# One diffusion-layer kernel: modulation of all tokens straight out of PSUM, the later modulation loads on GpSimd's queue, and more buffers for the stores of gates and values

## The chip, the cores and the metric

The kernel runs on one core of one Trainium2 chip. Five engines work side by side, each through its own list of instructions in order: PE (matrix multiplications and transposes, with PEld, the load of its stationary operand), DVE (vector), ACT (scalar, activations), POOL (GpSimd) and SP, which here only issues transfers. Transfers run on 16 DMA engines. The metric is the device time of one execution in microseconds, the median of several runs. Times inside a profile count from the start of the profiled span.

## The reference, cut to what matters

One layer of a diffusion backbone over 1024 latent tokens and 256 context tokens, in fp32. What the change touches is the front of the layer:

```python
mod_lat = (silu(c) @ w_ada + b_ada)[:, None, :]
mod_ctx = silu(c_ctx) @ w_ada + b_ada
sh1, sc1, gt1, sh2, sc2, gt2 = split(mod_lat, 6, axis=-1)
csh1, csc1, ... = split(mod_ctx, 6, axis=-1)
h_lat = rms_norm(x, norm_mix_g) * (1 + sc1) + sh1
h_ctx = rms_norm(ctx, norm_mix_g) * (1 + csc1) + csh1
y_lat, _ = token_mixer(h_lat, h_ctx, ...)   # h @ w_in -> attention and gated linear attention
x = x + gt1 * y_lat
x = x + gt2 * hier_moe(rms_norm(x, norm_ffn_g) * (1 + sc2) + sh2)
```

The projection h @ w_in gives, among other columns, the values of the gated linear attention (gv), its low-rank gates, keys and queries, the output gate r, and the values of the differential attention (dv).

## The kernel before, in words

Tokens stand in ten tiles of 128 (two of context, eight of latents), two to a pair: five pairs, pair 0 the context. An fp32 product is done as three matmuls of split operands (mm3, lines 119 to 121: high times high, low times high, high times low), so every weight w is split into whi (ACT, L275) and wlo (DVE, L276), and the modulated tokens, transposed to have the model dimension on partitions, into hThi and hTlo. A unit of work is one tile of tokens against one 256-column block of w_in: 24 matmuls into one of three PSUM tiles named acc.

The stages in order of time:

1. Modulation. The first 2048 columns of w_ada come as 16 pieces of 512 KB (wada, L385, SP's queue, AW = 4 buffers); ACT makes wadh (L390), DVE wadl (L391), PE multiplies (L397); ACT or DVE copy the rows out of PSUM (L406, L408), PE transposes them (L410), DVE forms modT (L435 to L437). Beside it, start_chain normalises pair 0 (its scaling is L340 on POOL), transposes it and copies the transposes from PSUM into xn (L315 on ACT, L317 on DVE).
2. Values. For each pair: squares (L297, ACT), the reciprocal root (L105 to L113, small steps of ACT and DVE), the scaling of the token tiles (L303, POOL), PE transposes in eight (L312), copies into xn (L317), and for each of eight blocks k of 128 model dimensions the modulation, done twice: ACT writes the rounded hThi (L324), POOL writes it unrounded over xn (L325), DVE subtracts (hTlo, L326). Then 20 units of gv: ACT copies acc out (gvs, L469) and SP's queue stores it (L470).
3. klr: keys and low-rank gates, 10 units.
4. r and q: 16 units of the output gate (gs, L703 to L709, stored at L710) and 8 of queries (ki, L723, which needs a load eP, L719; transposes L659). Beside it ada_rest computes the other 4096 columns of the modulation: 64 loads aw of 256 KB (L603, SP's queue, three buffers), one DVE step each which accumulates w times silu(c) into aacc (L645, L647), and for every 512 columns finish(j): the split of aacc into ah (ACT, L613) and al (DVE, L614), two matmuls against ones (L617, L618), the addition of the bias row brow (DVE, L619), and stores. The recurrence over the states sall (L589, L590) runs on DVE.
5. dv: 20 units whose result goes out as dqh (ACT, L864) and dql (DVE, L865), two buffers each, both stored from SP's queue. Then the rotary units, attention, output projection and the mixture of experts, up to the end at 1442 us.

The order on PE, ACT, DVE and POOL is written out by the program: chains are generators whose yields carry a delay (the table DEL), and a "Weave" lets them step when the unit loop has ticked that much. So an edit in a chain moves its instructions against those of the units. Transfers stand in the order in which their queue's engine reaches them; a load that waits for a free buffer holds what is queued behind it on that queue.

## Time and profile before

| | us |
|---|---|
| median of 3 runs | 1440.54 (1439.92 to 1441.53) |
| the profiled execution | 1444.24 |
| its span | 1442.4 |
| PE busy in the span | 1331.0 |
| DVE busy | 1115.2 |
| ACT busy | 870.6 |
| POOL busy | 298.7 |
| mean granted clock of PE | 0.967 |

The profile lists busy time by engine, groups of instructions by line, waits (which instruction stood idle until which other one ended) and a timeline. A share of busy time over the whole span is an average over stages with different limits, and so the windows by stage are to be read first. A granted clock of 1.00 is PE's upper level of 2.4 GHz, 0.50 the lower of 1.2 GHz.

### The profile page before, as it was taken

How to read it: one execution, taken by the hardware profiler on the slowest of the kernel's cores; microseconds unless marked ns; L12 is line 12 of the kernel's file. 1: busy time of each engine (PE TensorE's matmuls, PEld its weight loads, DVE VectorE, ACT ScalarE, POOL GpSimd, SP SyncE). 2: the span in 40 equal slices, each digit the busy share in tenths (PEclk: the TensorE clock that was granted, in tenths of full speed). 3: DMA queues.
4: the chain of work that ended last, by engine and by line, in shares of the span. 5: the costliest groups of instructions: out<-in, count | busy, mean ns of one | idle time of the engine just before them, and what ended most of it. 6: DMA issues, size and time to landing. Idle time of an engine off the chain costs nothing.

```text
span 1442.4 us, 21048 instructions
## 1 busy us (share of the span) xinstructions
PE 1331.0 (92%) x7352; PEld 1104.1 (77%) x7352; DVE 1115.2 (77%) x1653; ACT 870.6 (60%) x1458; POOL 298.7 (21%) x273
## 2 busy tenths in 40 slices
...
GB/s 262 202 96 150 199 220 186 249 244 183 175 174 178 265 152 18 141 36 112 220 254 138 263 311 355 375 368 369 373 372 377 374 368 354 366 371 359 347 294 151
DMA packets 121538, 360.76 MB, mean 250 GB/s; under 512 B 18726, under 2 KB 47422, under 8 KB 98388
## 3 DMA queue, kind: packets, MB, share of 16 engines
...
q8 instruction: 59, 0.97, 0.3%
q14 instruction: 51, 0.42, 0.1%
...
## 4 chain that ended last, share of the span: by engine, by line
PE 68%; DVE 13%; DMA 7%; ACT 5%; issue 4%; POOL 2%; SPq 0%; ACTq 0%; POOLq 0%; DVEq 0%
PE acc L119 5%; PE acc L120 5%; PE acc L121 5%; PE y L119 4%; PE y L121 4%; PE y L120 4%; PE u L120 4%; PE g L120 4%; PE u L121 4%; PE g L121 4%; PE g L119 4%; PE u L119 4%; PE y L1678 4%; DVE nm L1039 3%; PE S L1034 2%
## 5 line engine op out<-in xcount | busy, mean ns | idle before, releaser
L1630 DVE TENSOR_TENSOR lo<-ring,hi 128x1024 fp32r<-128x1024 f32 x323 | 382.5, 1221 | 42.5 <-ACT hi L1629 28.3
L1629 ACT ACTIVATE hi<-ring 128x1024 fp32r<-128x1024 f32 x323 | 335.7, 1059 | 86.9 <-PE y L121 54.2
L119 PE MATMUL acc<-whi,hThi 128*128 128x256 f32 (+1 forms) x592 | 175.6, 297 | 5.5 <-DVE dql L865 3.9
L121 PE MATMUL acc<-whi,hTlo 128*128 128x256 f32 (+1 forms) x592 | 170.0, 287 | 0.9 <-DVE hTlo L326 0.6
L120 PE MATMUL acc<-wlo,hThi 128*128 128x256 f32 (+1 forms) x592 | 169.9, 287 | 0.4 <-DVE wlo L276 0.3
L119 PEld LDWEIGHTS acc<-whi,hThi 128*128 128x128 f32 x592 | 115.2, 195 | 6.8 <-DVE dql L865 4.3
L120 PEld LDWEIGHTS acc<-wlo,hThi 128*128 128x128 f32 x592 | 114.9, 194 | 2.1 <-DVE wlo L276 0.8
L121 PEld LDWEIGHTS acc<-whi,hTlo 128*128 128x128 f32 x592 | 114.5, 193 | 2.4 <-DVE hTlo L326 2.1
L119 PE MATMUL g<-hi,xh 128*128 128x512 f32 x256 | 103.9, 406 | 0.1
L120 PE MATMUL u<-lo,xh 128*128 128x512 f32 x256 | 100.5, 393 | 3.1 <-DVE lo L1630 3.1
L119 PE MATMUL u<-hi,xh 128*128 128x512 f32 x256 | 100.6, 393 | 2.0 <-ACT hi L1629 2.0
L120 PE MATMUL g<-lo,xh 128*128 128x512 f32 x256 | 101.1, 395 | 0.8 <-DVE lo L1630 0.8
L121 PE MATMUL g<-hi,xl 128*128 128x512 f32 x256 | 101.2, 395 | 0.0
L121 PE MATMUL u<-hi,xl 128*128 128x512 f32 x256 | 100.3, 392 | 0.0
L1039 DVE TENSOR_REDUCE nm<-S 128x1 f32<-128x1280 f32 x64 | 94.8, 1484 | 6.1 <-PE S L1034 6.0
L1034 PE MATMUL S<-kst,qst 128*128 128x512 f32 (+1 forms) x384 | 92.0, 377 | 6.6 <-ACT p L1044 5.5
L1044 ACT ACTIVATE p<-S,nm 128x1280 f32<-128x1280 f32 x64 | 85.1, 1329 | 16.3 <-DVE nm L1039 11.1
L119 PE MATMUL y<-hi,th 128*128 128x512 f32 x186 | 85.2, 458 | 0.0
L1034 PEld LDWEIGHTS S<-kst,qst 128*128 128x128 f32 x384 | 65.3, 192 | 19.5 <-ACT p L1044 9.6
L1609 POOL DMA_INDIRECT xg<-dr_h,tok x32 | 45.1, 1411 | 151.7 <-ACT hi L1629 129.3
L121 PE MATMUL y<-hi,tl 128*128 128x512 f32 x186 | 72.6, 390 | 0.0
L120 PE MATMUL y<-lo,th 128*128 128x512 f32 x186 | 72.5, 390 | 0.0
...
## 6 DMA issues: line engine op xcount, KB each, us to landing
...
```

The lines of the kernel that those rows point to most:

```text
L119: nc.tensor.matmul(out_ap, ah, bh, start=start, stop=False)
L120: nc.tensor.matmul(out_ap, ah, bl, start=False, stop=False)
L121: nc.tensor.matmul(out_ap, al, bh, start=False, stop=stop)
L1034: nc.tensor.matmul(S[:, c0:c0 + cn], st["qst"][m][s][:, qt * P:(qt + 1) * P], st["kst"][m][:, c0:c0 + cn], start=(s == 0), stop=(s == 1))
L1039: nc.vector.tensor_reduce(d["nm"][:, m:m + 1], d["S"][m], AX.X, OP.max, negate=True)
L1044: nc.scalar.activation(d["p"][m], d["S"][m], AF.Exp, bias=d["nm"][:, m:m + 1], accum_out=d["sm"][:, m:m + 1])
L1609: nc.gpsimd.indirect_dma_start(out=xgb[e % 3], out_offset=None, in_=dr_h2, in_offset=bass.IndirectOffsetOnAxis(ap=tok[:, o:o + 1], axis=0) ...
L1629: nc.scalar.activation(hi, raw, AF.Copy)
L1630: nc.vector.tensor_tensor(lo, raw, f32(hi), op=OP.subtract)
L1678: nc.tensor.matmul(y[:, n], tf[:, kk - PARTS], ws[kk][:, n * 512:(n + 1) * 512], start=start, stop=stop)
```

## The change

- The loads of the first modulation part have 6 buffers (AW), the token tiles xt 6 (4 before).
- xn and its copies are gone. pair_transpose puts two blocks k of both tiles into one PSUM tile; DVE (36 times) or ACT (4 times, even k of pair 0) modulates from there into xm; pair_parts then copies xm into hThi on ACT and subtracts on DVE, both 512 wide. Pair 0 is transposed and modulated at the start of the value stage, behind modT.
- The scaling of the token tiles (L303) goes from POOL to ACT. The squares of pair 1 stand before rows 2 and 3 of the modulation, its scaling before the chains of the other pairs.
- The 64 loads aw are issued by GpSimd. In finish, the bias row is loaded there (one buffer), and a yield stands between ah and al.
- The small memset of st goes to DVE; gs has 4 buffers instead of 2; dqh and dql have 3, and in the dv stage two units share one, so that six units have room.

The first hunk, left out here, only sets AW from 4 to 6.

```diff
--- before.py
+++ after.py
...
@@ -283,11 +283,11 @@
     ada = ip.enter_context(ExitStack())
     ap = ada.enter_context(tc.tile_pool(name="ada", reuse_waits="tile", bufs=1))
     wv = io["w_ada"].rearrange("(p k) j -> p k j", k=KD)
-    xts, ssqs, xns = {}, {}, {}
+    xts, ssqs = {}, {}
 
     def tile_load(t):
         src = io["ctx"][t * P:(t + 1) * P] if t < NL else io["x"][(t - NL) * P:(t - NL + 1) * P]
-        xts[t] = ap.tile([P, D], F32, name="xt", bufs=4)
+        xts[t] = ap.tile([P, D], F32, name="xt", bufs=6)
         nc.sync.dma_start(xts[t], src)
 
     def tile_square(t):
@@ -297,33 +297,37 @@
         nc.scalar.activation(junk, xts[t], AF.Square, accum_out=ssqs[t // 2][:, t % 2:t % 2 + 1])
 
     def pair_scale(g):
-        *_, r = rsqrt(ap, ssqs[g], 1.0 / D, [P, 2], "n1")
+        *_, r = rsqrt(ap, ssqs[g], 1.0 / D, [P, 2], f"n1{g % 2}")
         for i in range(2):
             t = 2 * g + i
-            nc.gpsimd.tensor_scalar(xts[t], xts[t], r[:, i:i + 1], 1.0, op0=OP.mult, op1=OP.mult)
-
-    def tile_transpose(t, hb):
-        g = t // 2
-        if t % 2 == hb == 0:
-            xns[g] = ap.tile([P, KD, 256], F32, name="xn", bufs=3)
-        pt = pp.tile([P, 512], F32, name="t", bufs=DEL["T"])
-        for b in range(4):
-            k = hb * 4 + b
-            nc.tensor.transpose(pt[:, b * P:(b + 1) * P], xts[t][:, k * P:(k + 1) * P], ident)
-        dst = xns[g][:, hb * 4:hb * 4 + 4, t % 2 * P:t % 2 * P + P]
-        if hb and t < 4:
-            nc.scalar.activation(dst, pt.rearrange("p (b c) -> p b c", b=4), AF.Copy)
+            nc.scalar.activation(xts[t], xts[t], AF.Copy, scale=r[:, i:i + 1])
+
+    def modulated(g, k, dst, src):
+
+        c = 1 if 2 * g < NL else 0
+        sc, sh = modT[:, 1, k, c:c + 1], modT[:, 0, k, c:c + 1]
+        if g == 0 and k % 2 == 0:
+            nc.scalar.activation(dst, src, AF.Identity, scale=sc, bias=sh)
         else:
-            nc.vector.tensor_copy(dst, pt.rearrange("p (b c) -> p b c", b=4))
-
-    def pair_modulate(g, k):
-        c = 1 if 2 * g < NL else 0
-        sl = slice(2 * g * P, (2 * g + 2) * P)
-        sc, sh = modT[:, 1, k, c:c + 1], modT[:, 0, k, c:c + 1]
-        xn = xns[g][:, k]
-        nc.scalar.activation(hThi[:, k, sl], xn, AF.Identity, scale=sc, bias=sh)
-        nc.gpsimd.tensor_scalar(xn, xn, sc, sh, op0=OP.mult, op1=OP.add)
-        nc.vector.tensor_tensor(hTlo[:, k, sl], xn, f32(hThi[:, k, sl]), op=OP.subtract)
+            nc.vector.tensor_scalar(dst, src, sc, sh, op0=OP.mult, op1=OP.add)
+
+    def pair_transpose(g, kp):
+
+        pt = pp.tile([P, 2, 256], F32, name="t", bufs=DEL["T"])
+        for j in range(2):
+            for t in range(2):
+                k = 2 * kp + j
+                nc.tensor.transpose(pt[:, j, t * P:(t + 1) * P], xts[2 * g + t][:, k * P:(k + 1) * P], ident)
+        xm = ap.tile([P, 2, 256], F32, name="xm", bufs=2)
+        for j in range(2):
+            modulated(g, 2 * kp + j, xm[:, j], pt[:, j])
+        return xm
+
+    def pair_parts(g, kp, xm):
+
+        ks, sl = slice(2 * kp, 2 * kp + 2), slice(2 * g * P, (2 * g + 2) * P)
+        nc.scalar.activation(hThi[:, ks, sl], xm, AF.Copy)
+        nc.vector.tensor_tensor(hTlo[:, ks, sl], xm, f32(hThi[:, ks, sl]), op=OP.subtract)
 
     def start_chain():
 
@@ -339,29 +343,23 @@
         for t in range(2):
             nc.gpsimd.tensor_scalar(xts[t], xts[t], r[:, t:t + 1], 1.0, op0=OP.mult, op1=OP.mult)
         yield
-        yield
-        for t in range(2):
-            for hb in range(2):
-                tile_transpose(t, hb)
-                yield
 
     normed = [1]
 
     def pair_chain(g):
-        for t in (2 * g, 2 * g + 1):
-            tile_square(t)
-        pair_scale(g)
-        yield DEL["p0" if g > 1 else "pf"]
-        for t in (2 * g, 2 * g + 1):
-            for hb in range(2):
-                tile_transpose(t, hb)
-                yield DEL["p1" if g > 1 else "ph"]
-            if t + 4 < NA:
-                tile_load(t + 4)
-        for k in range(KD):
-            pair_modulate(g, k)
-            if k % 2:
-                yield DEL["p2" if g > 1 else "pg"]
+        if g > 1:
+            for t in (2 * g, 2 * g + 1):
+                tile_square(t)
+            pair_scale(g)
+            yield DEL["p0"]
+        for kp in range(KD // 2):
+            xm = pair_transpose(g, kp)
+            yield DEL["p1" if g > 1 else "ph"]
+            pair_parts(g, kp, xm)
+            yield DEL["p2" if g > 1 else "pg"]
+        for t in (2 * g + 6, 2 * g + 7):
+            if t < NA:
+                tile_load(t)
         normed[0] = g + 1
 
     with tc.manual_schedule():
@@ -430,16 +428,14 @@
                 next(wgen)
         for _ in chain:
             pass
+        for t in (2, 3):
+            tile_square(t)
         for n in range(2, 4):
             row(n)
         nc.vector.tensor_tensor(modT, pt[:, :, :, :2], bcol[:, :, :, None].to_broadcast([P, 2, KD, 2]), op=OP.add)
         nc.vector.tensor_tensor(modT, pt[:, :, :, 2:], modT, op=OP.add)
         nc.vector.scalar_tensor_tensor(modT[:, 1], modT[:, 1], 1.0,
                                        ncol[:, :, None].to_broadcast([P, KD, 2]), op0=OP.add, op1=OP.mult)
-        for k in range(KD):
-            pair_modulate(0, k)
-            if k % 2 and k < KD - 1:
-                next(wgen)
     dbg("modT", modT)
 
 
@@ -472,6 +468,13 @@
 
     side = Weave(DEL["w1"])
     with tc.manual_schedule(engines=COMPUTE):
+        for kp in range(KD // 2):
+            pair_parts(0, kp, pair_transpose(0, kp))
+            if kp < KD // 2 - 1:
+                next(wgen)
+        for t in (6, 7):
+            tile_load(t)
+        pair_scale(1)
         for g in range(1, NA // 2):
             side.add(pair_chain(g))
         for t0, t1 in ((0, 2), (2, 4), (4, NA)):
@@ -600,17 +603,20 @@
             i = len(ws)
             if i < 8 * KD:
                 ws.append(sp.tile([P, 512], F32, name="aw", bufs=3))
-                nc.sync.dma_start(ws[i], wv[:, i % KD, 2048 + i // KD * 512:2048 + (i // KD + 1) * 512])
+                nc.gpsimd.dma_start(ws[i], wv[:, i % KD, 2048 + i // KD * 512:2048 + (i // KD + 1) * 512])
 
         for _ in range(3):
             load()
         accs = {}
 
         def finish(j):
-            acc, brow = accs.pop(j)
+            acc = accs.pop(j)
+            brow = sp.tile([1, 512], F32, name="brow", bufs=1)
+            nc.scalar.dma_start(brow, io["b_rest"][:, j * 512:(j + 1) * 512])
             ah = sp.tile([P, 512], F32R, name="ah", bufs=1)
             al = sp.tile([P, 512], F32R, name="al", bufs=1)
             nc.scalar.activation(ah, acc, AF.Copy)
+            yield DEL["ar2"]
             nc.vector.tensor_tensor(al, acc, f32(ah), op=OP.subtract)
             yield DEL["ar2"]
             ps = pp.tile([P, 512], F32, name="t", bufs=DEL["T"])
@@ -635,9 +641,7 @@
 
         for j in range(8):
             acc = sp.tile([P, 512], F32, name="aacc", bufs=2)
-            brow = sp.tile([1, 512], F32, name="brow", bufs=2)
-            accs[j] = (acc, brow)
-            nc.scalar.dma_start(brow, io["b_rest"][:, j * 512:(j + 1) * 512])
+            accs[j] = acc
             for k in range(KD):
                 w = ws[j * KD + k]
                 c = sil[:, 0, k:k + 1]
@@ -687,7 +691,7 @@
             if t == 0:
                 nc.scalar.preload_act_table_set("natural_log_exp_and_others")
             st = sp.tile([P, 98], F32R, name="st", bufs=3)
-            nc.gpsimd.memset(f32(st[:, 96:98]), 1.0)
+            nc.vector.memset(f32(st[:, 96:98]), 1.0)
             nc.scalar.activation(st[:, 0:32], ps[:, 256:288], AF.Copy)
             nc.scalar.activation(st[:, 64:96], ps[:, 256:288], AF.Copy)
             nc.vector.tensor_tensor(st[:, 32:64], ps[:, 256:288], f32(st[:, 0:32]), op=OP.subtract)
@@ -699,7 +703,7 @@
         for i in range(2):
             for t in range(NT):
                 ps = bform(f"r{i}", NL + t)
-                gs = sp.tile([P, 256], F32, name="gs")
+                gs = sp.tile([P, 256], F32, name="gs", bufs=4)
                 nc.scalar.activation(gs, ps[:, :256], AF.Exp, scale=-1.0)
                 nc.scalar.activation(gs, gs, AF.Ln, bias=1.0)
                 nc.scalar.activation(gs, gs, AF.Exp, scale=-1.0)
@@ -805,8 +809,8 @@
 
     def evacuate(h, qk, c0, cn, ps):
 
-        hi = sp2.tile([P, 512], F32R, name="dqh")[:, :cn]
-        lo = sp2.tile([P, 512], F32, name="dql")[:, :cn]
+        hi = sp2.tile([P, 512], F32R, name="dqh", bufs=3)[:, :cn]
+        lo = sp2.tile([P, 512], F32, name="dql", bufs=3)[:, :cn]
         sc = 1.0 if qk else 0.125
         src = ps[:, :cn]
         if c0:
@@ -859,8 +863,9 @@
         for i in range(2):
             for t in range(NA):
                 ps = bform(f"dv{i}", t)
-                hi = sp2.tile([P, 512], F32R, name="dqh")[:, :256]
-                lo = sp2.tile([P, 512], F32, name="dql")[:, :256]
+                if t % 2 == 0:
+                    pair = [sp2.tile([P, 512], dt, name=nm, bufs=3) for nm, dt in (("dqh", F32R), ("dql", F32))]
+                hi, lo = [x[:, t % 2 * 256:t % 2 * 256 + 256] for x in pair]
                 nc.scalar.activation(hi, ps[:, :256], AF.Copy)
                 nc.vector.tensor_tensor(lo, ps[:, :256], f32(hi), op=OP.subtract)
                 nc.sync.dma_start(dr_v[i][0][:, t], f32(hi))
```

**ACT at the end of the modulation stage.** Before (wadh is a piece's high part, xn the copied transposes of pair 0, junk the squares of pair 1, wada the copied rows of the modulation):

```order
L390 ACTIVATE wadh<-wada 128x1024 x3
L315 ACTIVATE xn<-t 128x4x128
L390 ACTIVATE wadh<-wada 128x1024 x2
L315 ACTIVATE xn<-t 128x4x128
L390 ACTIVATE wadh<-wada 128x1024 x7
L406 ACTIVATE wada<-acc 4x512
L275 ACTIVATE whi<-wraw 128x512
L406 ACTIVATE wada<-g 4x512
L297 ACTIVATE junk,ssq<-xt 128x1024 x2
```

After:

```order
L388 ACTIVATE wadh<-wada 128x1024 x12
L404 ACTIVATE wada<-acc 4x512
L275 ACTIVATE whi<-wraw 128x512
L297 ACTIVATE junk,ssq<-xt 128x1024 x2
L404 ACTIVATE wada<-g 4x512
L310 ACTIVATE xm<-t,modT 128x256
```

The two xn copies between the wadh steps are gone, and the two squares moved ahead of the second copy of a row.

**PE at the start of the value stage.** Before (acc_474 is the first unit, acc_544 the second; t the transposes, here of pair 1):

```order
L119 MATMUL acc_474<-whi_449,hThi_154 128x256
L120 MATMUL acc_474<-wlo_450,hThi_154 128x256
L121 MATMUL acc_474<-whi_449,hTlo_155 128x256
L119 MATMUL acc_544<-whi_412,hThi_154 128x256
L120 MATMUL acc_544<-wlo_413,hThi_154 128x256
L121 MATMUL acc_544<-whi_412,hTlo_155 128x256
L312 MATMUL t_549<-ident_60,xt_356 128x128 x4
L119 MATMUL acc_544<-whi_412,hThi_154 128x256
```

After (xt_189 is of pair 0; xt_331 and xt_333 are pair 1; acc_485 is the first unit):

```order
L320 MATMUL t_460<-ident_60,xt_189 128x128
L119 MATMUL acc_485<-whi_387,hThi_154 128x256
L120 MATMUL acc_485<-wlo_388,hThi_154 128x256
L121 MATMUL acc_485<-whi_387,hTlo_155 128x256
L320 MATMUL t_489<-ident_60,xt_331 128x128
L320 MATMUL t_489<-ident_60,xt_333 128x128
L320 MATMUL t_489<-ident_60,xt_331 128x128
L320 MATMUL t_489<-ident_60,xt_333 128x128
L119 MATMUL acc_485<-whi_387,hThi_154 128x256
```

The first transposes of pair 1 moved from behind 27 unit matmuls to behind three.

**DVE from the last ki to the first dql.** Before (brow is the addition of a bias row):

```order
L723 TENSOR_TENSOR ki<-eP,acc 128x512
L645 SCALAR_TENSOR_TENSOR aacc<-aw,sil,aacc 128x512
L614 TENSOR_TENSOR al<-aacc,ah 128x512
L619 TENSOR_TENSOR brow<-t,brow 1x512
L645 SCALAR_TENSOR_TENSOR aacc<-aw,sil,aacc 128x512 x3
L614 TENSOR_TENSOR al<-aacc,ah 128x512
L619 TENSOR_TENSOR brow<-t,brow 1x512
L754 COPY st_in<-sall 64x512
L755 COPY st_in<-sall 64x512
L865 TENSOR_TENSOR dql<-acc,dqh 128x256
```

After:

```order
L727 TENSOR_TENSOR ki<-eP,acc 128x512
L625 TENSOR_TENSOR brow<-t,brow 1x512
L637 SCALAR_TENSOR_TENSOR ah<-brow,al 1x64x8
L649 SCALAR_TENSOR_TENSOR aacc<-aw,sil,aacc 128x512 x3
L651 TENSOR_SCALAR aacc<-aw,sil 128x512
L649 SCALAR_TENSOR_TENSOR aacc<-aw,sil,aacc 128x512 x4
L620 TENSOR_TENSOR al<-aacc,ah 128x512
L625 TENSOR_TENSOR brow<-t,brow 1x512
L649 SCALAR_TENSOR_TENSOR aacc<-aw,sil,aacc 128x512 x3
L620 TENSOR_TENSOR al<-aacc,ah 128x512
L625 TENSOR_TENSOR brow<-t,brow 1x512
L758 COPY st_in<-sall 64x512
```

Eleven steps of aacc now stand between the last ki and the first dql, where four stood.

## Rows read from the trace of the kernel before

**Rows 1.** Windows by stage: length, busy us (instructions) of PE, PEld, DVE, ACT, POOL; clock, DMA

```profile
20.00:43.60 23.60, 17.08 (x74) 6.20 (x72) 15.72 (x19) 14.09 (x19) 0.23 (x1) 0.92 0.84 292
43.60:122.00 78.40, 72.09 (x550) 69.12 (x551) 38.01 (x87) 42.36 (x93) 40.77 (x51) 0.89 0.41 129
...
186.00:288.00 102.00, 87.91 (x713) 83.62 (x713) 86.13 (x144) 41.43 (x90) 1.95 (x3) 0.97 0.72 220
288.00:475.00 187.00, 183.51 (x1122) 162.99 (x1121) 104.47 (x240) 47.58 (x145) 46.96 (x32) 0.99 0.62 191
```

**Rows 2.** Waits, modulation stage: who waited for whom; total us, times, longest

```profile
DVE wadl L391 <- ACT wadh L390: 5.9, 5, 2.2
ACT xn L315 <- PE t L312: 5.9, 2, 4.4
```

**Rows 3.** Timeline of DVE, modulation stage: start, us, line, instruction, [idle before]

```profile
28.34 3.63 DVE L391 TENSOR_TENSOR wadl<-wada,wadh 128x1024 fp32r<-128x1024 f32 x3 [0.99 <-ACT wadh L390]
...
38.40 1.23 DVE L391 TENSOR_TENSOR wadl<-wada,wadh 128x1024 fp32r<-128x1024 f32 x1 [0.20 <-ACT wadh L390]
...
43.35 0.17 DVE L437 SCALAR_TENSOR_TENSOR modT<-modT,c_ncol 128x16 f32<-128x16 f32 x1
```

**Rows 4.** Groups by line, value stage: instructions xcount | busy us, mean ns | idle before

```profile
L325 POOL TENSOR_SCALAR xn<-xn,modT 128x256 f32<-128x256 f32 x40 | 30.8, 784 | 31.8 <-ACT hThi L324 31.8
L324 ACT ACTIVATE hThi<-xn,modT 128x256 fp32r<-128x256 f32 x40 | 20.8, 588 | 0.0
...
L317 DVE COPY xn<-t 128x512 f32<-128x512 f32 x14 | 9.3, 685 | 3.1 <-PE t L312 3.1
```

**Rows 5.** Timeline of ACT at the end of the modulation stage

```profile
41.23 1.04 ACT L297 ACTIVATE junk<-xt 128x1024 f32<-128x1024 f32 x1
```

**Rows 6.** Timeline of POOL in the value stage

```profile
45.76 6.32 POOL L325 TENSOR_SCALAR xn<-xn,modT 128x256 f32<-128x256 f32 x6 [0.17 <-ACT hThi L324]
...
95.35 6.19 POOL L325 TENSOR_SCALAR xn<-xn,modT 128x256 f32<-128x256 f32 x8 [1.02 <-ACT hThi L324]
```

**Rows 7.** Timeline of PE where the second pair's transposes begin

```profile
54.27 1.11 PE L312 MATMUL t<-ident,xt 128*128 128x128 f32 x4 [0.46 <-POOL xt L303]
```

**Rows 8.** Windows at low granted clock (columns as in rows 1)

```profile
44.00:56.70 12.70, 11.14 (x39) 9.09 (x40) 6.22 (x18) 9.07 (x22) 9.86 (x10) 0.50 0.24 68
84.00:87.40 3.40, 3.40 (x18) 3.40 (x18) 1.04 (x2) 1.75 (x4) 2.42 (x4) 0.50 0.14 43
```

**Rows 9.** Waits in the stage of gates and queries

```profile
PE t L618 <- DVE al L614: 5.1, 4, 2.6
...
PE t L617 <- ACT ah L613: 2.9, 3, 1.5
```

**Rows 10.** Timeline of DVE around the last ki and the first dql

```profile
278.21 0.69 DVE L723 TENSOR_TENSOR ki<-eP,acc 128x512 f32<-128x512 f32 x1 [2.58 <-DMA eP<-dr_eP]
...
282.93 0.75 DVE L645 SCALAR_TENSOR_TENSOR aacc<-aw,sil,aacc 128x512 f32<-128x512 f32 x1 [0.16 <-DMA aw<-in_w_ada_dram]
...
287.10 0.42 DVE L865 TENSOR_TENSOR dql<-acc,dqh 128x256 f32<-128x256 f32 x1
...
295.40 0.43 DVE L865 TENSOR_TENSOR dql<-acc,dqh 128x256 f32<-128x256 f32 x1 [6.35 <-ACT dqh L864]
```

**Rows 11.** Timeline of SP's queue in the same stretch

```profile
279.58 0.33 SPq L603 DMA_DIRECT2D aw<-in_w_ada_dram  x1
```

**Rows 12.** Line 161: a plain load issued by GpSimd (durations min/median/max, ns)

```profile
L161 POOL DMA_DIRECT2D ring<-in_w_up_dram x1: 614/614/614, 823.2 to 823.2; - x1
```

**Rows 13.** Line 1609, GpSimd's gathers: time to landing

```profile
DMA to landing us min/median/max: 5.2/12.2/13.5
```

**Rows 14.** Waits in the first units of dv

```profile
PE acc L119 <- DVE dql L865: 3.9, 2, 2.6
```

2 lines of the change are left out of this document (1 added, 1 removed).

## The prediction, made before the changed kernel ran

> **What bounds the kernel now.** I read the table by stage first [rows 1]: PE is busy 72.09 of the 78.40 us of the value stage, 87.91 of the 102.00 us of the stage of gates and queries (r and q), and 183.51 of 187.00 us behind that. So nothing the diff does before 288 us changes what comes after; it only moves it. The places where time can come or go are the 23.60 us ahead of the value stage, in which neither PE (17.08) nor DVE (15.72) nor ACT (14.09) is full and the DMA engines are at 0.84; the value stage's start; and r/q, where DVE is busy 86.13 us, almost as much as PE, so that taking away a wait of PE alone buys little there.
>
> The times: the profiled execution took 1444.24 us with a span of 1442.4; the median of the three timed runs is 1440.54. All terms below are differences inside the span, and I add their sum to the median. A difference of 0.2% (2.9 us) is about what a measurement of this kernel can tell from none.
>
> **The modulation's first part (A).** The list of waits [rows 2] shows ACT standing 5.9 us in front of two copies of transposes (L315), one of them 4.4, with the next wadh behind it, and DVE waiting 5.9 us for wadh. Undisturbed, DVE does three pieces in 3.63 us, 1.21 each [rows 3]; its last piece starts at 38.40 and modT is ready at 43.52. The change takes the two ACT copies, their two DVE twins (0.685 each) [rows 4] and the transposes out of this stretch, and gives the loads six buffers. At most that is 5.9 + 2 x 0.685 = 7.3 us for the last piece; the nine pieces that DVE starts behind 23 us, at 1.22 each, would end near 34.5 instead of 39.6, 5.1 us less, and the DMA share of 0.84 says that the loads can hardly give more. Against it, the two squares of pair 1 (L297, 1.04 us each [rows 5]) now stand ahead of ACT's second copy of a modulation row, on the path to modT: +0.3 to +1.2, since PE's transposes of the row before run beside the first. I take **-4.7**, with -6 (squares hidden) and -3 (loads landing too late for six buffers to matter fully) as ends.
>
> **The value stage (B).** What the change removes is large and lies beside other work: 40 modulations on GpSimd (30.8 us), 40 ACT writes (20.8) [rows 4], 8 scalings on GpSimd and 40 DVE subtractions. In their place stand 36 modulations on DVE and 4 on ACT, 20 ACT copies and 20 DVE subtractions of double width, and 8 scalings on ACT (a 128x1024 ACT pass is 1.04 [rows 5]). ACT comes out a few us lighter, DVE one or two heavier, each still near half busy. So what counts is the path. Before, the first pair went at GpSimd's pace: six of its eight steps in 6.32 us [rows 6], the pair done 9 us after modT. After, each of four steps is ACT's modulation and copy, DVE's subtraction and split of a weight, then the next one: 0.6 + 0.6 + 0.7 + 0.7, with overlap 2.3 or so, the fourth done 8.8 us after modT. No gain.
>
> The second pair is worse placed. Before, its transposes stand behind 27 matmuls, and waited 0.46 us for the scaled tokens at 54.27, 10.75 us after modT [rows 7]. After, they stand behind three. The scalings wait on ACT behind the whole first pair, two small ACT steps with three of DVE between, and take 1.04 each: done 11.6 to 12.3 us after modT. There PE stands with 21 matmuls of its first unit behind it: at the half clock of that stretch (0.50; elsewhere at 0.50 PE did 18 in 3.40 us, 0.19 each [rows 8]) they are 4.0 us, at the full one 2. Later pairs repay some, since GpSimd no longer holds DVE's subtractions (PE ran at half clock from 84 to 87.4 us behind one such wait [rows 8]). Pairs that come 12.6 us apart make the last pair ready about 60.4 us after modT, against 58.5 (GpSimd's last step of it ends at 101.54 [rows 6], and one subtraction of DVE follows), with seven units behind it either way. I take **+4**; ends +1 (only the later transposes, the rest repaid) and +7 (all 21 matmuls at half clock and half the later gap again). A and B together are about -0.7: the start's gain is handed back by a pair 1 that is scaled too late.
>
> **Gates and queries (D).** The loads aw leave SP's queue, where each waited for its buffer and held the stores and loads behind it. On GpSimd's queue only the two zeroings (L853, L855) stand behind the 64 loads, and their first reader comes with the dv stage: nothing. On PE the new yield between ah and al covers the 5.1 and 2.9 us that L618 and L617 waited [rows 9]. But those were waits on a DVE that is nearly full; PE freed of them meets DVE's ki and gs a little later. What remains is DVE's own count. The order puts 43 accumulations of aacc between the first gate and the first dql, before 40, and 7 additions of brow, before 6: 3 x 0.68 + 0.6 = **+2.6**. The wait of ki for eP (2.58 us [rows 10]) had its load queued among aw loads on SP; it goes: **-2.6**.
>
> Then the tail. Before, 8.9 us lie between the last ki (278.21) and the first dql (287.10), with four accumulations [rows 10]. After, eleven stand there, eight in a row. They are the unknown of this change, for three buffers turn no faster than a load comes: on SP, the load that was issued at 279.58, as its buffer came free [rows 11], was waited for and used at 282.93 [rows 10]: 3.35 us. With three buffers a clump runs at (R + 0.74)/3 us a piece, R being that round trip: 1.37 instead of 0.74, times eight is 5.0 us, less some 2 us in which al and brow fill the wait. So **+3** at SP's R. The trace has two plain loads issued by GpSimd, which took 0.6 us of that engine [rows 12], which is below 0.74 and so no limit; and gathers of 512 KB which landed after 5.2 us at the least [rows 13]. R = 2.25 gives 0, R = 5.2 gives +8: the ends. I take SP's value, as the nearest row of the same size and layout.
>
> The Trainium skill, "DMA: Bandwidth & Descriptors", section "Anatomy of one DMA — SWDGE (gpsimd) path", gives 2.0 us plus bytes at 436 GB/s; by that estimate 256 KB would take 2.6 us, the tail would cost +1 instead of +3, and the forecast would be 2 us lower. No run here shows it.
>
> **Values (E).** The units of dv stored through two buffers; DVE stood 6.35 us and the first dql after it came at 295.40 [rows 10], PE having waited 2.6 us for one [rows 14]. Six units of room cover that: **-2.6**. What is late next is PE itself, full from there on [rows 1].
>
> **Clock (F).** PE will stand longer at one place, about 10 us in front of the fourth dv unit, whose PSUM buffer the first dql frees. After its gap before 84 us PE ran 3.4 us at 0.50 [rows 8], which at full clock would be 1.7. I take **+1.5**, 0 to 3.4. The klr stage keeps its order: 0, plus or minus 1.
>
> Sum: -4.7 + 4 + 2.6 - 2.6 + 3 - 2.6 + 1.5 = +1.2, so 1440.5 + 1.2 = **1441.7 us**.
>
> **The rivals.**
> Faster (1): pair 1's scaling is not what PE waits for, or is repaid at once (B = +1), and the loads land at R = 2.25 to 2.6 (tail 0 to +1). Then -4.7 + 1 - 2.6 + 0.5, with D's 2.6 against 2.6 and no clock loss, is -5.8; with a half of PE's 8 us at L617 and L618 paid back it is -10. About 1433. For it: each wait named was real in the trace. Against it: DVE's 86 of 102 us.
>
> Slower (2): loads issued by GpSimd come back late. At R = 4 us the tail costs +4.7 and the sum is +2.9, the point from which this case decides; at 5.2 it is +8, and the accumulations spread over r/q, which lie 1.5 to 2 us apart, wait as well above R = 4.5: some +3. 1441.7 - 3 + 8 + 3 is about 1450. For it: the gathers' 5.2 [rows 13]; against it: they run among the weight streams. The Trainium skill, "SBUF — State Buffer", section "Who interferes with whom", speaks for it: DVE copies and tensor_scalar in a two-port mode block GpSimd's writing of descriptors until they end. By rows here few such instructions stand in the tail (one start of an accumulator per eight), so alone it is a delay of half a microsecond.
>
> Not what it says (3): the first stage is paced by its DMA, and six buffers and freer engines bring 1.5 us instead of 4.7. Then 1445.
>
> **How the numbers follow.** The balance as summed, 1437.5 to 1446: 0.43; rival 1: 0.26; rival 2: 0.23; rival 3: 0.08. Of the balance, 0.29 lies within 0.2%, 0.03 below and 0.11 above; rival 1 is faster but for 0.02; rival 2 slower but for 0.02; rival 3 splits 0.02 and 0.06. Faster 0.27, same 0.35, slower 0.38. The range reaches into rivals 1 and 2 to about their middles: 1432 to 1451; the likeliest case alone is 1437.5 to 1446.
>
> **What would show it.** In the profile after: modT ready near 39 us (A; near 42 speaks for rival 3); PE idle before the first pair-1 transposes, and the last gvs some 81 to 83 us after modT (B; 78 or less refutes it); no wait of PE at L618 and none of ki for eP (D); waits of aacc for DMA aw bunched in the last 18 us before the first dql, and the time from a buffer's release to its next use: 3.3 us for me, under 2.6 for rival 1, over 4 for rival 2; no 6 us hole before a dql in dv (E); a half-clock stretch near 290 (F). The prediction is wrong if r/q shortens with PE, by more than 4 us, or if the first dql comes before 283 us or after 292.

## The result, and the profile after

The changed kernel is slower: 1454.10 us in the median of six runs (1448.37 to 1456.43) against 1440.59 before. The ratio is 1.0078 with a 95% interval of 1.0060 to 1.0096, that is 11.2 us; the two medians lie 13.5 us apart. Its profiled execution took 1451.38 us with a span of 1449.6. Forecast were 1441.7 us, 1.2 above before, with a range of 1432 to 1451 and a chance of 0.38 for slower.

Table by stage of the changed kernel, cut at its own places: behind modT, at the last gvs, the last ki, the first dql and the first score of the attention (columns as in [rows 1]):

```profile
20.00:39.60 19.60, 14.44 (x69) 5.04 (x66) 14.43 (x16) 13.40 (x16) 2.42 (x4) 0.96 0.93 330
39.60:125.70 86.10, 71.31 (x557) 68.98 (x558) 42.92 (x90) 43.80 (x83) 1.08 (x2) 0.89 0.35 111
189.50:279.60 90.10, 78.06 (x633) 74.26 (x631) 75.40 (x127) 37.51 (x82) 17.16 (x32) 0.97 0.66 205
279.60:300.70 21.10, 11.46 (x85) 9.86 (x83) 12.94 (x20) 4.94 (x10) 6.19 (x11) 0.82 0.60 191
300.70:483.90 183.20, 181.85 (x1113) 162.09 (x1114) 103.67 (x239) 45.71 (x141) 45.30 (x31) 0.99 0.62 195
```

Set beside the kernel before, the profiled times of the same events say where the time went:

| | before | after | change of the stretch |
|---|---|---|---|
| modT ready | 43.52 | 39.57 | -3.95 |
| last gvs (behind modT) | 121.96 (78.44) | 125.70 (86.12) | +7.68 |
| first gate gs | 185.69 | 189.54 | +0.11 |
| last ki ends | 278.89 | 279.59 | -3.15 |
| first dql | 287.10 | 300.66 | +12.86 |
| first score of the attention | 472.81 | 483.88 | -2.49 |
| sum | | | +11.06 |

Two stretches lose: the value stage, and what lies between the last ki and the first dql, where PE is busy 11.46 of 21.1 us at a granted clock of 0.82. Behind the first score nothing was changed, and the runs of one kernel differ there by some microseconds either way (the rest took 969.6 us before and 965.7 after, in one execution each, and 962 to 971 over the profiles of all kernels here). So the two profiled executions are only 7.1 us apart (1444.24 and 1451.38), and that the sum of the table comes near the 11.2 us of the ratio is in part chance.

DVE's timeline of the changed kernel behind its last ki (answers to [rows 10]; start, us, line, instruction, idle time before it):

```profile
281.90 1.09 DVE L637 SCALAR_TENSOR_TENSOR ah<-brow,al 1x512 f32<-1x512 f32 x1 [1.46 <-DMA al<-in_ffn_g_dram]
...
286.85 0.49 DVE L651 TENSOR_SCALAR aacc<-aw,sil 128x512 f32<-128x512 f32 x1 [1.72 <-DMA aw<-in_w_ada_dram]
...
290.64 0.75 DVE L649 SCALAR_TENSOR_TENSOR aacc<-aw,sil,aacc 128x512 f32<-128x512 f32 x1 [1.00 <-DMA aw<-in_w_ada_dram]
...
297.80 0.69 DVE L620 TENSOR_TENSOR al<-aacc,ah 128x512 fp32r<-128x512 f32 x1 [0.76 <-ACT ah L618]
...
300.66 0.42 DVE L870 TENSOR_TENSOR dql<-acc,dqh 128x256 f32<-128x256 f32 x1
...
306.14 0.42 DVE L870 TENSOR_TENSOR dql<-acc,dqh 128x256 f32<-128x256 f32 x1 [2.60 <-ACT dqh L869]
```

DVE goes from one short wait to the next: for the load of the norm's gain (1.46), for aw, for ah. The first dql is 13.6 us later than in [rows 10], and behind the 292 us that the prediction named as the latest. PE's timeline at that place, its three long waits in a row:

```profile
293.45 0.39 PE L624 MATMUL t<-al,ones 128*1 128x512 f32 x1 [3.96 <-DVE al L620]
297.83 0.59 PE L623 MATMUL t<-ah,ones 128*1 128x512 f32 x1 [3.98 <-ACT ah L618]
...
301.14 0.58 PE L119 MATMUL acc<-whi,hThi 128*128 128x256 f32 x1 [2.00 <-DVE dql L870]
```

PE has filled the three PSUM tiles of the dv units by then (the last product starts at 289.22), and only finish's small matmuls are left to it. ACT's order shows why the tiles stay full: the last ah stands there ahead of the first dqh, and it waits 11.35 us for the accumulations. In the kernel before the same wait was 3.42 us, and the first dqh began at 284.69.

```profile
297.14 0.63 ACT L618 ACTIVATE ah<-aacc 128x512 fp32r<-128x512 f32 x1 [11.35 <-DVE aacc L649]
...
298.05 0.39 ACT L869 ACTIVATE dqh<-acc 128x256 fp32r<-128x256 f32 x1 [0.28 <-issue]
```

The list of waits between 190 and 305 us (answers to [rows 9]):

```profile
DVE aacc L649 <- DMA aw<-in_w_ada_dram: 10.2, 11, 2.5
...
PE t L624 <- DVE al L620: 7.5, 4, 4.0
...
PE t L623 <- ACT ah L618: 4.0, 1, 4.0
...
DVE aacc L651 <- DMA aw<-in_w_ada_dram: 1.7, 1, 1.7
```

DVE waits 11.9 us for aw (7.4 ahead of the last ki, 4.5 behind it), where before it waited 3.9; and PE's waits at the two matmuls of finish, which the yield was to cover, are 11.5 us instead of 8.0. GpSimd issues the load that DVE waits for at 286.85 as follows (start, us, idle time before it), and below stands the time from issue to landing of the 64 loads on its queue:

```profile
283.85 0.54 POOL L606 DMA_DIRECT2D aw<-in_w_ada_dram  x1 [5.62 <-DVE aacc L649]
...
DMA to landing us min/median/max: 2.8/3.5/6.8
```

In the value stage, the rows of PE at its start (answers to [rows 7]) show the wait for pair 1's scaled tokens (51.25). It ends 11.7 us after modT, where 11.6 to 12.3 was forecast:

```profile
38.32 0.59 PE L408 MATMUL g<-ident,wada 4*128 4x4 f32 x4 [1.62 <-ACT wada L404]
40.90 1.09 PE L320 MATMUL t<-ident,xt 128*128 128x128 f32 x4 [1.99 <-DVE xm L312]
43.35 1.09 PE L320 MATMUL t<-ident,xt 128*128 128x128 f32 x4 [1.36 <-DVE xm L312]
...
51.25 0.47 PE L320 MATMUL t<-ident,xt 128*128 128x128 f32 x1 [6.17 <-ACT xt L303]
```

### The profile page after: what moved, and what is told of

Same layout as the page of the kernel before. It is cut to its first block, busy times and chain, and to the rows that moved or that the text cites. A ratio compares the mean times of both kernels' runs of the same rounds, so it can differ in the third digit from the quotient of the medians.

```text
span 1449.6 us, 20984 instructions
## 1 busy us (share of the span) xinstructions
PE 1326.4 (92%) x7352; PEld 1101.1 (76%) x7352; DVE 1119.0 (77%) x1663; ACT 870.7 (60%) x1446; POOL 291.3 (20%) x279
## 4 chain that ended last, share of the span: by engine, by line
PE 48%; DMA 18%; issue 18%; DVE 10%; POOL 4%; ACT 2%; POOLq 0%; SPq 0%; ACTq 0%; DVEq 0%
DMA ring<-in_w_up_dram 3%; DMA raw_o<-in_w_up_dram 3%; DMA aw<-in_w_ada_dram 3%; PE y L119 3%; PE y L121 3%; PE y L120 3%; PE u L120 3%; PE u L121 3%; PE u L119 3%; DVE nm L1044 3%; PE g L119 3%; PE g L121 3%; PE g L120 3%; PE y L1683 2%; PE S L1039 2%
## 5 line engine op out<-in xcount | busy, mean ns | idle before, releaser
L1634 ACT ACTIVATE hi<-ring 128x1024 fp32r<-128x1024 f32 x323 | 335.8, 1059 | 86.1 <-PE y L121 53.9
L120 PE MATMUL u<-lo,xh 128*128 128x512 f32 x256 | 101.4, 396 | 3.7 <-DVE lo L1635 3.7
L119 PE MATMUL g<-hi,xh 128*128 128x512 f32 x256 | 103.2, 403 | 0.1
L1049 ACT ACTIVATE p<-S,nm 128x1280 f32<-128x1280 f32 x64 | 85.0, 1328 | 18.3 <-DVE nm L1044 13.6
L606 POOL DMA_DIRECT2D aw<-in_w_ada_dram x64 | 34.6, 541 | 238.5 <-DVE aacc L649 129.1
```

The source lines that it names most:

```text
L119: nc.tensor.matmul(out_ap, ah, bh, start=start, stop=False)
L120: nc.tensor.matmul(out_ap, ah, bl, start=False, stop=False)
L606: nc.gpsimd.dma_start(ws[i], wv[:, i % KD, 2048 + i // KD * 512:2048 + (i // KD + 1) * 512])
L1049: nc.scalar.activation(d["p"][m], d["S"][m], AF.Exp, bias=d["nm"][:, m:m + 1], accum_out=d["sm"][:, m:m + 1])
L1634: nc.scalar.activation(hi, raw, AF.Copy)
```

## The experiments

All ratios are to the kernel before, run beside the experiment on the same chip, with 95% intervals. "The stretch" is the time from the end of the last ki to the first dql (before 8.2 us, after 21.1), "the stage" the time from the first gs to the first dql (before 101.4, after 111.1).

### Which part of r and q loses: the yield, the queue, or the buffers

**e1_aw_sp**, the changed kernel with

```diff
-                nc.gpsimd.dma_start(ws[i], wv[...])
+                nc.sync.dma_start(ws[i], wv[...])
```

> The changed kernel with the 64 aw loads back on SP's queue; nothing else. Theory T (the order: the yield in finish puts eleven accumulations behind the last ki, and three buffers cannot feed a clump): the same clump stands there, fed at a round trip of about 3.3 us instead of 3.7, so from the last ki to the first dql 19 to 21 us as in the changed kernel (21.1), and the time 1 us or less below it, or above it, since the eP loads queue behind aw again. Theory Q (loads issued by GpSimd come late, and that is the loss): the stretch falls to 13 us or less and the time by 6 to 9 us.

Measured: 1.0093 (1.0074 to 1.0113), 1456.24 us; stretch 20.4, stage 108.1. DVE's waits for aw fall from 11.9 to 7.1 us, and the time does not follow. Theory Q falls.

**e2_no_yield**, the changed kernel with

```diff
             nc.scalar.activation(ah, acc, AF.Copy)
-            yield DEL["ar2"]
             nc.vector.tensor_tensor(al, acc, f32(ah), op=OP.subtract)
```

> The changed kernel without the new yield between ah and al; the loads stay on GpSimd. Theory T: four accumulations behind the last ki as before the change, the stretch to the first dql 8 to 10 us instead of 21.1; the seven accumulations now ahead of the last ki cost 5 us there, so the first dql about 293 instead of 300.7, and the time falls by 6 to 8 us; PE's waits at the two matmuls of finish come back and cost nothing. Theory Q: the aw waits of DVE (10.2 us in the stage) stay and only move; the time falls by 3 us at most.

Measured: 0.9987 (0.9971 to 1.0003), 1442.45 us; stretch 10.5, stage 104.0, first dql at 294.31. One line carries the whole loss: 1.0078 against 0.9987 is 13 us, more than the 6 to 8 of theory T. Of these, the two profiles show 8.8 between the first gs and the first score (294.3 us against 285.6). The windows up to the last ki and behind it, to be held against the third and fourth row of the changed kernel:

```profile
190.30:283.80 93.50, 80.30 (x646) 76.73 (x644) 78.98 (x132) 38.92 (x84) 19.91 (x38) 0.96 0.69 217
283.80:294.30 10.50, 8.49 (x67) 7.85 (x67) 6.32 (x10) 3.37 (x8) 2.66 (x5) 1.00 0.59 199
```

DVE does 6.3 us of work in the stretch instead of 12.9, and PE's clock stays at 1.00.

**e9_yield_only**, the kernel before with that yield alone (loads on SP).

> The kernel before with the yield between ah and al alone (aw on SP, value stage as before). If the yield is the cause by itself: eleven accumulations behind the last ki, the stretch to the first dql 19 to 21 us instead of 8.2, the time 8 to 12 us above before. If it is bad only together with GpSimd's queue: 13 us or less in that stretch and the time within 4 us of before.

Measured: 1.0076 (1.0056 to 1.0095), 1451.37 us; eleven accumulations behind the last ki, stretch 19.7, stage 109.0. The yield costs about as much (11 us) without any other part of the change. Its windows:

```profile
183.40:272.70 89.30, 76.50 (x639) 72.72 (x638) 75.55 (x128) 37.47 (x83) 1.95 (x3) 1.00 0.68 210
272.70:292.40 19.70, 10.49 (x79) 8.70 (x77) 12.84 (x21) 4.04 (x8) 0.00 (x0) 0.86 0.58 190
```

**e6_sp_no_yield**, both edits: no yield, and the loads on SP.

> The changed kernel without the new yield and with the aw loads back on SP: the queue's price under the old order. If GpSimd's queue costs by later loads (its DVE waits for aw were 8.8 us with this order on GpSimd, its load takes 0.5 us of GpSimd), DVE's waits for aw fall to 4 to 5 us, the stretch from the last ki to the first dql from 10.5 to 8 to 9 us, and the time by 1 to 3 us against the kernel without the yield. If the queue is worth what the change says (SP no longer blocked behind aw), the wait of ki for eP returns and the time rises by 1 to 3 us.

Measured: 1.0043 (1.0023 to 1.0062), 1445.65 us; stretch 8.4, stage 103.2; waits for aw 5.0 us, and the wait of ki for eP is back with 3.4. The second outcome, against e2_no_yield's 0.9987: with this order GpSimd's queue does not lose, it gains.

**e14_pool_only**, the kernel before with the loads on GpSimd and the small memset on DVE.

> The kernel before with the 64 aw loads on GpSimd's queue alone (and the small memset of st on DVE, as in the change, so that it does not stand between them). If the queue change by itself costs (later loads), DVE's waits for aw rise from 3.6 to 8 us or more in the stage, the first dql comes 2 to 4 us later and the time rises by 2 to 4. If it frees SP, the wait of ki for eP (2.6) goes and the time falls by 2 to 4. If both, within 1.5 us of before.

Measured: 0.9970 (0.9952 to 0.9988), 1438.48 us. DVE's waits for aw rise from 3.9 to 9.8 us and the wait of ki for eP is gone; the stage takes 103.1, which is 1.7 more than before. So the gain of 4 us is measured, but the profile of one execution does not show it in this stage; where it lies stays open.

**e17_yield01**, the changed kernel with the yield's delay cut:

```diff
-            yield DEL["ar2"]     (1.84)
+            yield 0.1
```

> The changed kernel with the new yield's delay at 0.1 instead of 1.84. Six accumulations stand behind the last ki instead of eleven (four without the yield). If the delays' sum is the cause, the stretch from the last ki to the first dql is 12 to 14 us (21.1 with 1.84, 10.5 without) and the time 7 to 10 us below the changed kernel, 0 to 3 us above the one without the yield. If the yield as such is the cause, the time stays within 4 us of the changed kernel.

Measured: 1.0028 (1.0011 to 1.0045), 1447.76 us; six accumulations behind the last ki, stretch 13.4, stage 107.4. With almost no delay the yield still loses nearly half: 7 us below the changed kernel as the first outcome has it, but 6 above the one without the yield.

**e10_yield_ar**, the kernel e7_start (below, without the yield) with the yield back and the other delay cut:

```diff
-            DEL: 'ar': 1.15
+            DEL: 'ar': 0.95
...
+            yield DEL["ar2"]
```

> The kernel e7_start with the yield between ah and al back, and the delay of each accumulation (ar) cut from 1.15 to 0.95, so that the 64 accumulations give back the 13 ticks that seven yields add: three accumulations behind the last ki, as many as without the yield. If the loss was the sum of delays (the chain ending late and clumped), the stretch from the last ki to the first dql stays at 10 us or less and the time within 2 us of e7_start, or below it by up to 4 if PE's 8.4 us of waits at the second matmul of finish were worth something. If the yield itself is bad (al later, brow later), the stretch is above 13 us and the time 4 us or more above e7_start.

Measured: 1.0027 (1.0009 to 1.0044), 1447.95 us, where e7_start is at 0.9982. Neither outcome came as written: the time is 6.5 us above e7_start, as with a yield that is bad by itself, but the stretch is short. It is 5.3 us, with two accumulations in it; instead the stage takes 106.5 instead of 104.1, and the stage ahead of it (klr) 65.8 instead of 63.2. PE's wait at finish's second matmul fell from 8.4 to 2.8 us and gave nothing. So the stretch is the form that the loss takes, not its only one: with the accumulations earlier, PE waits 6.4 us for DVE's gs (0.2 in e7_start) and 5.7 for its ki (2.7). No run has the shorter delay ar without the yield, so what of this comes from the delay is open.

**e12_aw4**, the changed kernel with

```diff
-                ws.append(sp.tile([P, 512], F32, name="aw", bufs=3))
+                ws.append(sp.tile([P, 512], F32, name="aw", bufs=4))
...
-                gs = sp.tile([P, 256], F32, name="gs", bufs=4)
+                gs = sp.tile([P, 256], F32, name="gs", bufs=2)
```

> The changed kernel with 4 buffers for aw instead of 3 (and gs back at 2 to make room), order untouched. With four buffers a clump turns at (R + 0.75)/4: at R = 3.6 that is 1.09 us a piece instead of 1.45. The waits of DVE for aw behind the last ki (4.5 us) fall to about 1.5, the stretch to the first dql from 21 to 18 us, the time by 2 to 4. If the waits are nothing to the result (PE and ACT pace the stretch through ah, al and brow), the stretch stays above 20.

Measured: 1.0029 (1.0015 to 1.0043), 1448.36 us; stretch 17.8, stage 107.0, waits for aw 2.4 us. DVE's waits for aw were on the path, and more so than the 2 to 4 us expected: 7 us in time, 4.1 in the stage of the one profile. (The two buffers fewer for gs are part of this edit.)

**e16_e7_aw4**, e7_start with the same two lines.

> The kernel e7_start with 4 buffers for aw and 2 for gs. With only four accumulations behind the last ki, if DVE's waits for aw (7.8 us in e7_start's stage) are on the path, they fall below 3 us and the time by 2 to 4 us below e7_start (1438.7, 0.9982 of before). If PE's matmuls pace the stage ahead of the last ki, the waits go and the time stays within 1 us.

Measured: 0.9918 (0.9896 to 0.9940), 1431.67 us; stage 97.2 instead of 104.1. Waits in that stage, e7_start first, then with four buffers:

```profile
PE t L626 <- DVE al L622: 8.4, 4, 4.1
DVE aacc L651 <- DMA aw<-in_w_ada_dram: 6.4, 5, 2.4
...
DVE aacc L653 <- DMA aw<-in_w_ada_dram: 1.4, 1, 1.4
```

```profile
PE t L626 <- DVE al L622: 3.9, 5, 1.3
...
DVE aacc L651 <- DMA aw<-in_w_ada_dram: 1.0, 1, 1.0
```

One buffer takes away 6.8 us of DVE's waits, 4.5 of PE's, and 6.9 us of the stage. In time, 0.9918 against 0.9982 is 9 us, where 2 to 4 were expected.

**e19_before_aw4**, the kernel before with four buffers for aw, the room coming from one bias row instead of two (loaded in finish, no yield).

> The kernel before with 4 buffers for aw and the bias row loaded in finish; the loads stay on SP, where each holds what is queued behind it. If the buffers alone are worth it (DVE's waits for aw, 3.9 us, go), the time falls by 2 to 4 us. If SP's queue sets the loads' times whatever the buffers, it stays within 1.5 us.

Measured: 0.9957 (0.9943 to 0.9970), 1436.23 us; stage 96.8. That is 6.2 us in time and 4.6 in the stage (101.4 before), where 2 to 4 were expected; DVE no longer waits for aw. Three buffers held back r and q in the kernel before already. (The bias row's later load is part of this edit and was not measured alone.)

### The value stage

**e3_pf**, the changed kernel with

```diff
             pair_scale(g)
             yield DEL["p0"]
+        else:
+            yield DEL["pf"]
         for kp in range(KD // 2):
```

> The changed kernel with a yield (pf, as before the change) ahead of pair 1's transposes, so that 27 unit matmuls stand before them instead of 3. Theory V (PE's wait of 6.2 us at those transposes, with 21 matmuls it could have done behind it, is what the value stage lost): the wait falls below 2 us, the last gvs comes 3 to 4 us earlier (122 instead of 125.7), and the time falls by 3 to 4. Rival W (the pairs become ready when they do, and PE only waits elsewhere): pair 1 is ready at 67.8 us or later as now, the wait moves behind the first unit, and the last gvs moves by less than 1 us.

Measured: 1.0082 (1.0055 to 1.0109), 1453.57 us; last gvs at 126.15, 85.9 behind modT. PE's timeline in the first 25 us of the stage:

```profile
49.49 0.39 PE L119 MATMUL acc<-whi,hThi 128*128 128x256 f32 x1 [0.98 <-ACT hThi L329]
...
51.93 0.33 PE L320 MATMUL t<-ident,xt 128*128 128x128 f32 x1 [0.64 <-ACT xt L303]
...
59.35 0.39 PE L119 MATMUL acc<-whi,hThi 128*128 128x256 f32 x1 [2.91 <-ACT whi L275]
...
63.03 0.58 PE L119 MATMUL acc<-whi,hThi 128*128 128x256 f32 x1 [1.20 <-ACT whi L275]
```

The wait is cut into smaller ones at other instructions: PE now stands 2.91 and 1.20 us for weights whose split (whi) follows pair 2's squares and scaling on ACT (52.82 to 58.41). Rival W holds: the order on PE was not the cause. (Its ratio is not to be told from the 1.0078 of the changed kernel.)

**e5_scale_pool**, the changed kernel with pair_scale(1) on GpSimd, moved up:

```diff
         for t in (2, 3):
             tile_square(t)
+        pair_scale(1)     (g == 1: nc.gpsimd.tensor_scalar, else ACT)
         for n in range(2, 4):
             row(n)
...
-        pair_scale(1)
```

> The changed kernel with pair 1 scaled on the idle GpSimd, from its squares on, ahead of the modulation's last rows, instead of on ACT behind the whole first pair. Theory V: pair 1's tokens are ready near 43 us, PE's 6.2 us wait is gone or under 1, pair 1 is done 5 us earlier (62 to 63 instead of 67.8), the last gvs near 121, the time 4 to 5 us below the changed kernel; modT comes up to 0.7 us later. Rival W: the later pairs are paced by ACT and DVE and the last gvs moves by 1 us or less although pair 1 is early.

Measured: 1.0050 (1.0028 to 1.0073), 1450.14 us. The wait of 6.2 us is gone, the last gvs comes 83.1 us behind modT instead of 86.1; but modT came at 42.79, since squares and scaling wait for their tokens ahead of the second row copy. The time is about 4 us better, but the two intervals overlap, so this gain is not shown; the place of the last gvs is unmoved (125.92). Behind modT 3 of the 4 to 5 us of theory V come, and the late modT takes them back.

**e7_start**: e2_no_yield with the row copies ahead of the squares again, and pair_scale(1) on GpSimd right behind modT.

> The changed kernel without the new yield, with the row copies of the modulation ahead of pair 1's squares again, and pair 1 scaled on GpSimd right behind modT. Theory: the 15 us of gaps of PE in the value stage are what it lost, since PE is full from 89 us on; modT comes at 37 to 38.5 us instead of 39.6 to 41, the 6.2 us wait at pair 1's transposes falls to 2 or less, the last gvs comes at 120 to 121.5 instead of 125.7 to 127, and the time is 4 to 6 us below the kernel without the yield, 3 to 6 us below the kernel before. Rival: other waits in the value stage take the place of this one, and the last gvs stays above 124.

Measured: 0.9982 (0.9973 to 0.9992), 1438.69 us; modT at 37.23, last gvs at 120.74, 83.5 behind it. Faster than before, by 2.6 us. The places came as the theory has them, the last gvs 6.3 us ahead of e2_no_yield's 127.07. The time did not: 4 to 6 us below the kernel without the yield were expected, and 0.9982 against 0.9987 is 0.7, with overlapping intervals. PE still waits at the start, in the chain of pair 0; the first wait is put down to a step of pair 1's reciprocal root, which stands among pair 0's steps on DVE:

```profile
38.82 1.09 PE L323 MATMUL t<-ident,xt 128*128 128x128 f32 x4 [2.25 <-DVE n_t L109]
42.14 1.08 PE L323 MATMUL t<-ident,xt 128*128 128x128 f32 x4 [2.24 <-DVE xm L315]
...
44.59 1.08 PE L323 MATMUL t<-ident,xt 128*128 128x128 f32 x4 [0.72 <-DVE xm L315]
```

**e13_g**, e10_yield_ar with

```diff
-        pt = pp.tile([P, 2, 256], F32, name="t", bufs=DEL["T"])
+        early = g == 0 and kp > 1
+        pt = pp.tile([P, 2, 256], F32, name="g" if early else "t", bufs=DEL["G" if early else "T"])
```

> The kernel e10_yield_ar with the last two of pair 0's four transpose tiles in PSUM tiles of the other name (g), which stand free there, so that PE need not wait for DVE to empty t. If PE's two waits of 2.2 us in front of them are part of what the value stage lost, the first unit ends earlier, and the last gvs comes 1.5 to 3 us sooner after modT (81 instead of 83.5). If pair 0's loop over ACT and DVE paces the unit, the waits move into the unit's matmuls and the last gvs moves by less than 0.7.

Measured: 1.0032 (1.0018 to 1.0046), the same as e10_yield_ar's 1.0027; the two waits at the transposes go, 1.6 and 0.8 us at hThi and hTlo take their place, and the last gvs comes 82.5 us behind modT instead of 84.3. The waits move as the second outcome has it, the 1.8 us in the place is nearer the first, and the time shows nothing.

### The parts that gain

**e8_dv_only**, the kernel before with the dv hunks alone.

> The kernel before with one part of the change alone: dqh and dql with 3 buffers, two dv units to one. The hole of DVE of 6.35 us and PE's waits of 3.9 us at dql go; the stage from the first dql to the 20th takes 63 to 64 us instead of 66.5 and the time falls by 2.5 to 3.9. Rival: PE, freed there, is throttled or waits for weights behind it, and the time stays within 1 us.

Measured: 0.9990 (0.9976 to 1.0005), 1440.92 us. From the first dql to the first score it took 181.6 us instead of 185.7, from the first dql to the 20th 62.3 instead of 66.5. PE's waits at dql fall from 3.9 to 1.3 us. The mechanism is in the main as expected; in the time it doesn't show beyond noise.

**e11_dv_aw5**, e8_dv_only with AW = 5.

> The kernel e8_dv_only (before, with the dv buffers) with 5 buffers for the first modulation loads instead of 4 (6 do not fit beside xn): the part of the start's gain that is buffers. If the loads wait for buffers, modT comes 1.5 us or more earlier (41.6 in e8_dv_only, 40 or less here); if the xn copies on ACT and DVE set the pace, it moves by less than 0.7 us, and the time by nothing that can be measured.

Measured: 0.9975 (0.9963 to 0.9987), 1440.51 us; modT at 41.17 against 41.59. This one comparison is within the scatter of one start. Over the builds, DVE's last piece ended at 38.0 to 39.6 us with 4 buffers (five profiles, mean 38.8), at 37.3 to 38.0 with 5 (three, 37.5), and at 34.3 to 35.8 with 6 and the copies gone (seven, 34.9). By these means the fifth buffer gave 1.3 us, the sixth and the copies 2.6.

**e15_pool_dv_aw5**, e11_dv_aw5 with the loads on GpSimd as in e14_pool_only.

> The kernel before with the parts of the change that did not lose alone: the dv buffers, 5 buffers for the first loads, aw on GpSimd. If the parts add up, 0.25% to 0.6% below before (e11_dv_aw5 was at 0.9975), 1433 to 1438 beside 1441 to 1443. If the queue costs here, at or above e11_dv_aw5.

Measured: 0.9966 (0.9947 to 0.9984), 1437.95 us: at the weak end of what was expected. The gains of e14_pool_only (0.30%) and e11_dv_aw5 (0.25%) would add to 0.55%, measured are 0.34%; the interval nearly reaches the sum.

**e18_all**, e15_pool_dv_aw5 with four buffers for aw and the bias row in finish.

> The kernel before, its value stage untouched, with the parts that gained: aw on GpSimd with 4 buffers, the bias row loaded in finish (one buffer, no yield), the memset of st on DVE, dv buffers, 5 buffers for the first loads. e16 (0.9918) had its last gvs at 122.6, the old value stage at 117.6 to 120.4; if the parts add up the time is 2 to 5 us below e16, 0.988 to 0.991. If a stage gives back what another gained, it is at e16 or above.

Measured: 0.9915 (0.9898 to 0.9932), 1429.27 us, by the ratio 12.3 us below the kernel before (by the medians 14.7). By ratio it is not to be told from e16_e7_aw4, though its last gvs came 2.5 us earlier (120.1 against 122.6), so whether the old value stage or the mended new one is better stays open.

## Why the prediction was wrong, step by step

**A, modT earlier: right, smaller than thought.** Forecast -4.7, -3.95 in the two profiles. But starts scatter: five profiles with the old start have modT at 41.1 to 43.5 (mean 42.1), seven with the changed one at 39.6 to 41.0 (mean 40.4), and that is -1.8. The near hit of the two profiles is luck: its kernel before has the latest start of the five, its changed one the earliest of the seven. DVE's last piece came 3.9 us earlier by the same means (forecast 5.1), so rival 3, a stage paced by its loads, falls, though its -1.5 is near the mean. Besides these 1.2 us, the step that was mis-sized is the pair of squares: from the last piece to modT it took 3.3 us with the old order and 5.4 with the new, +2.1 where +0.3 to +1.2 was forecast. In the changed kernel the two squares and the waits for their tokens' loads (0.57 us) take ACT from 34.92 to 37.70, with the row copy behind; PE's row at 38.32 waits 1.62 us for that copy. With the copy ahead, e7_start took 3.2 us again and had modT at 37.2.

**B, the value stage: right in sign and place, too small.** Forecast +4 with an end at +7, measured +7.7 (eight profiles with the old value stage took 77.2 to 80.2 us from modT to the last gvs, six with the new one unaltered 85.8 to 86.3). The wait at pair 1's transposes was forecast and measured (6.2 us). The prediction gave two reasons for it: the place in PE's order, and a scaling that comes late on ACT. The first was wrong by e3_pf; the second holds for the place of the last gvs (e5_scale_pool and e7_start get 3 us back behind modT), while in time no gain of it is shown. What failed is the term for the later pairs, which were to lose 1.9 us and to repay some of it. A pair is ready when DVE ends its last hTlo: 9.0, 26.2, 39.1, 51.4 and 58.5 us after modT before, 9.9, 28.2, 41.9, 55.2 and 64.4 after (60.4 was forecast for the last), so the delay grows from pair to pair, from 0.9 to 5.9 us. One place where it grows is ACT's order behind pair 0: pair 2's squares and scaling stand there between pair 1's scaling and its first copy into hThi.

```profile
52.14 1.04 ACT L297 ACTIVATE junk<-xt 128x1024 f32<-128x1024 f32 x1
...
55.64 2.19 ACT L303 ACTIVATE xt<-xt,n_y 128x1024 f32<-128x1024 f32 x2 [0.62 <-DVE n_y L113]
57.73 0.61 ACT L329 ACTIVATE hThi<-xm 128x512 fp32r<-128x512 f32 x1
```

In the whole stage ACT's copies into hThi stood 22.1 us for xm. In e7_start pair 1 is no later than before (25.9) and the last pair still 3.3 us late (61.8); no run separates ACT's part in that from DVE's. Rival 1 falls with this term.

Groups by line in the changed kernel's value stage (answers to [rows 4]):

```profile
L312 DVE TENSOR_SCALAR xm<-t,modT 128x256 f32<-128x256 f32 x36 | 18.0, 537 | 4.8 <-PE t L320 4.2 <-ACT xm L310 0.6
L330 DVE TENSOR_TENSOR hTlo<-xm,hThi 128x512 fp32r<-128x512 f32 x20 | 13.8, 691 | 18.9 <-ACT hThi L329 18.9
...
L329 ACT ACTIVATE hThi<-xm 128x512 fp32r<-128x512 f32 x20 | 12.6, 629 | 22.1 <-DVE xm L312 22.1
...
L303 ACT ACTIVATE xt<-xt,n_y 128x1024 f32<-128x1024 f32 x8 | 8.8, 1142 | 2.8 <-DVE n_y L113 2.8
```

**D, gates and queries: the step that failed.** Forecast +3.0 (work +2.6, eP -2.6, tail +3), measured +9.7 from the first gs to the first dql. The work was counted right: DVE's busy time is 88.34 us in the two stretches of the changed kernel and 85.53 in the same two of the kernel before, +2.8. DVE's idle time was not: from 15.9 to 22.9 us, +7.0, where +0.4 was forecast. Two errors are in it. First, the prediction took DVE for nearly full, so that work which moves behind the last ki should come off ahead of it, and the wait for eP too. 3.9 us of DVE's work went, and 3.15 us of time; but the sum had also counted on 2.6 for eP. That wait did go, and the waits for aw (11.9 us in all instead of 3.9) ate it up: DVE's idle time ahead of the last ki went from 13.9 to 14.7 us. Second, behind the last ki DVE is idle for 8.2 us, where it was 2.0 and 3 more were forecast: 4.5 for aw, 1.5 for the gain's load, the rest in the turns of ah, al and brow, while PE has nothing else to do and ACT's last ah holds the first dqh. Nor did the yield cover PE's waits at finish, as forecast: they rose from 8.0 to 11.5 us. The forecast saw the eleven accumulations and the three buffers, and took the clump's price alone. It did not ask whether the three buffers held the stage back already; e19_before_aw4 says that they did, by 6 us in time. DVE's 86 of 102 us, read as "nearly full", were 86 with 16 of waits, of which the rows put only 3.9 down to aw.

**The cause in the code** is the yield: taken out, the time comes back (e2_no_yield, 13 us); put alone into the kernel before, it is lost (e9_yield_only, 11 us). The delays' sum is part of it (e17_yield01 still loses nearly half with a delay of 0.1), and the clump seems not to be all (e10_yield_ar has none and loses 6 us, with another delay changed too). How the rest divides between al's later place and ACT's and PE's order is not settled.

**Rival 2**, slower at 1450, had the sign and the place, not the mechanism. Its point was R of 4 us or more; R is what was forecast (3.3 us): the load issued at 283.85 was used at 286.85, 3.3 us after its buffer had come free at 283.58, and the median to landing is 3.5. SP's queue instead of GpSimd's changes nothing with the yield (e1_aw_sp) and loses without (e6_sp_no_yield). The Trainium skill's estimate of 2.6 us ("DMA: Bandwidth & Descriptors", "Anatomy of one DMA — SWDGE (gpsimd) path") lies below all 64 loads, of which the quickest took 2.8. Of the blocking that the Trainium skill tells of ("SBUF — State Buffer", "Who interferes with whom") the trace of the changed kernel shows no sign: an issue took GpSimd 0.54 us in the median and 0.75 at most, beside a DVE that was busy most of the time. But few of DVE's instructions there are copies or tensor_scalar (L651 stands five times among some 147), so this is a weak test.

**E and F** were right in sign; E was larger. E alone is -4.2 (e8_dv_only), forecast -2.6. F is +1.7 to +3.0, forecast +1.5: with the new dv buffers and the yield at 1.84, 183.2 to 184.5 us lie between the first dql and the first score in seven profiles, without the yield 181.5 in seven of eight (183.1 in e6_sp_no_yield). In the changed kernel the cause is as forecast: PE's granted clock is at the lower level, 0.50, for 10.2 us from its long waits on. 3.7 of these lie behind the first dql, which by halves is a loss of some 1.9 us (an estimate).

```profile
294.20:304.40 10.20, 4.44 (x17) 3.42 (x18) 7.53 (x14) 3.11 (x7) 1.32 (x3) 0.50 0.66 223
304.40:330.00 25.60, 25.60 (x209) 25.18 (x209) 9.91 (x29) 5.76 (x19) 0.00 (x0) 1.00 0.86 272
```

It is not the whole of F: e10_yield_ar and e13_g take 183.3 us as well, with the clock at 1.00 and PE busy throughout in the first 44 us behind the first dql. What it is there stays open.

**The klr stage**, forecast at 0 plus or minus 1, was right: +0.1.

In the sum: -0.7 for A and B became +3.7, +3.0 for D became +9.7, -1.1 for E and F became -2.5.
